# VectorE order in FF1: weight sums of a pair nearer to the pair, second-weight sums tied to the pairs' positions

## The chip, the cores and the metric

One Trainium2 chip, one of its cores. The metric is the device time of one execution in microseconds (us), lower is better. The kernel before took 1879.66 us (median of 3 runs, 1875.06 to 1884.38).

## The reference

One decoder layer on a sequence of 1024 tokens and a width of 1024. The first sublayer mixes tokens (sliding-window attention and a gated delta rule, side by side), the second is an MLP with 4096 hidden features. The change lies in the MLP's first product; everything ahead of it and the second product behind it are only neighbours.

```python
x = layer_norm(ALPHA * x + (1.0 + gt1) * mixed, ln1_g, ln1_b)     # end of the first sublayer
u2 = x * (1.0 + sc2) + sh2
h = jnp.square(jax.nn.relu(u2 @ w_ff1 + b_ff1))                    # FF1: (1024 x 1024) @ (1024 x 4096)
x = layer_norm(ALPHA * x + (1.0 + gt2) * (h @ w_ff2 + b_ff2), ln2_g, ln2_b)   # FF2
```

All of it is float32 from inputs to output.

## The kernel before, in words

**Number format.** Each float32 operand is split into a high part (ScalarE copies it to the matmul's type, line 215) and a low part (VectorE subtracts the high part from the source, line 216). A product is the sum of three matmuls: high by high, high by low, low by high.

**FF1 by seven products.** FF1 works on 16 pairs. Pair `i` is the two blocks of 128 hidden features `i` and `i + 16`. The product of 2 x 2 blocks (two halves of the 1024 inputs, two blocks of features, two halves of the tokens) is made from seven block products instead of eight, in the manner of Strassen and Winograd. That needs sums and differences of the weight blocks ahead of the products, and of the results behind them. Each product is 12 matmuls (4 slices of 128 by 3 split parts), so FF1 has 16 x 7 x 12 = 1344 matmuls of 128x512 on line 1869. From pair 5 on the products of a pair run in the order 1, 2, 6, 5, 7, 3, 4, and a pair takes 84 matmuls. Pairs 0 to 4 (`EARLY = 5`) are interleaved: products 1 and 2 of all five run first, then five products for each.

**Accumulators.** Products 1, 6, 7 and 4 of a pair add up in one PSUM bank (`mm`), 5 and 3 in another (`b`), product 2 has a third (`a`); in the first five pairs other banks take these parts. Because intermediate sums of a bank are results of their own, a bank is read in the middle: after product 5 ScalarE reads `b` (`part`, line 1587) before product 3 may go on in it, and after product 7 VectorE reads `mm` (`full`, line 1545) before product 4 may go on in it. TensorE waits at exactly these places when the reader is late.

**Results.** `part` copies a bank with the bias into a tile `t` (six of them rotate); `full` adds a bank to such a tile; `square` (lines 1595 and 1596) applies relu and square and stores the tile to `hf_d` in HBM through ScalarE's DMA queue; `last_block` (1606, 1607) does the same for product 4. `h_sums` and `h_sums2` (rows `sa`, `t`, `sb` on VectorE) make the sums of results that FF2 needs.

**First weights.** For each pair `f_load` (line 1541, SyncE's queue) brings two blocks of 512 KB (`fraw`). `f_alpha` splits the first as it is. Then `f_sums` makes `x` and an in-place sum (2 VectorE rows of 128x512), `f_sums2` makes two more in place (2 rows), and `f_gamma`, `f_beta`, `f_delta` split the changed blocks and `x`. Alpha serves products 1 and 2, gamma 6 and 3, beta 5 and 4, delta 7.

**Second weights.** FF2 uses seven products too. The sums of its weights are made during FF1: `t_load(n)` (lines 1691 to 1693, GpSimd's queue) loads 1 MB into `wx` (two tiles) and half of `sb`, `t_make(n)` makes four differences on VectorE (rows `wx<-wx` x3 and `sb<-sb,wx`, 128x512 each) and stores 4 x 256 KB to `wt_d` (line 1703, GpSimd's queue). There is one set of these buffers, so `t_load(n + 1)` writes where `t_make(n)` stored from.

**What sets the order.** The kernel writes every engine's queue itself. `at(p, f, ...)` puts an action at position `p`, and all actions up to `p` are written into the queues just ahead of the matmul with that number. `F0` is the number of FF1's first matmul, `pos[i, m]` that of product `m` of pair `i`. A position sets only the order of rows on an engine, not a time: each engine takes its rows strictly in that order, and waits for whatever a row depends on. Below, `b` is the position at which a pair begins, `pos[i, 1]`.

Of the kernel before, what the change touches and what calls it, by code (L numbers as in the profile page):

```python
# [34 lines left out]
def hybrid_layer_kernel(ctx: ExitStack, tc: tile.TileContext,  # L35
# [11 lines left out]
    V, A, G, T = nc.vector, nc.scalar, nc.gpsimd, nc.tensor  # L47
# [94 lines left out]
    NPAIR, EARLY = NF // 2, 5  # L142
# [54 lines left out]
    def at(p, f, *args):  # L197
        order[0] += 1
        heapq.heappush(events, (p, order[0], f, args))
# [325 lines left out]
    with tc.tile_pool(name="pa", bufs=2, side="right") as pa:  # L525
        if True:
            ba = pv.tile([P, NT, 16], F32, name="ba")
            for t in range(NT):
# [14 lines left out]
                if t:  # L543
                    vd = pa.tile([P, 4, 64], F32, tag="vd", name="vd", bufs=1)
                    a, b = (vraw, pv4) if t % 2 == 0 else (pv4, vraw)
# [106 lines left out]
        for h in range(8):  # L652
# [7 lines left out]
            for half in range(2):  # L660
                tp = psum("c", 1) if half else psum("b", 2)
                for j in range(4):
                    n = 4 * half + j
                    T.transpose(tp[:, j * P:(j + 1) * P], kT[:, n * P:(n + 1) * P], ident)
                for j in range(4):
                    n = 4 * half + j
# [16 lines left out]
            for half in range(2):  # L683
                kk = psum("a", 2)
                for j in range(4):
                    n = 4 * half + j
                    kc = kT[:, n * P:(n + 1) * P]
                    T.matmul(kk[:, j * P:(j + 1) * P], lhsT=kc, rhs=kc, start=True, stop=True)
                for j in range(4):
                    n = 4 * half + j  # L690
# [545 lines left out]
    for h in range(8):  # L1236
        b = Q0 + 144 * h
# [108 lines left out]
    F0 = E0 + 4 * SEG  # L1346
# [298 lines left out]
    pos = {im: F0 + 12 * n for n, im in enumerate(seq)}  # L1645
# [13 lines left out]
    for i in range(1, NPAIR):  # L1659
        if i < EARLY:  # L1660
            b = pos[i, 5]
            at(b - 70, f_load, i)
            at(b - (26 if i == 1 else 40), f_sums, i, V)
            at(b - (25 if i == 1 else 36), f_sums2, i, V)
            at(b - 17, f_beta, i)
            at(b - 3, f_gamma, i)
            at(b + 10, f_delta, i)
        else:
            b = pos[i, 1]
            at(b - 104, f_load, i)  # L1670
            at(b - (34 if i == EARLY else 76), f_alpha, i)
            at(b - (28 if i == EARLY else 66), f_sums, i, V)
            at(b - (27 if i == EARLY else 60), f_sums2, i, V)
            at(b + (8 if i == EARLY else -34), f_gamma, i)
            at(b + (26 if i == EARLY else -9), f_beta, i)
            at(max(b - (0 if i == EARLY else 22), pos[i - 1, 7] + 13), f_delta, i)
    for i in range(NPAIR):
# [25 lines left out]
            nc.gpsimd.dma_start(out=wt_d[j, n], in_=t)  # L1703

    for n in range(NPAIR):
        at(F0 + 110 + 76 * n, t_load, n)
        at(F0 + 146 + 76 * n, t_make, n)

# [117 lines left out]
    for s in range(7 * NS):  # L1828
        p = G0 + 24 * s
# [25 lines left out]
    for i, m in seq:  # L1855
# [8 lines left out]
        for k in range(4):  # L1864
            for x_ in range(3):
                run_events(count[0])
                (wh, wl), (uh_, ul_) = WF[i, w], U[mv]
                a, b = ((wh, uh_), (wh, ul_), (wl, uh_))[x_]
# [139 lines left out]
```

## Time and profile before

| | |
|---|---|
| time, median of 3 runs | 1879.66 us (1875.06 to 1884.38) |
| the profiled execution | 1881.81 us, of which the span from first to last instruction is 1880.1 us |
| TensorE clock granted, mean over the span | 0.990 |
| FF1's 1344 matmuls | from 1240.9 to 1561.0 us of the span |
| VectorE busy in the span | 1306.0 us (69%) |
| ScalarE busy in the span | 977.6 us (52%) |

All further times are microseconds from the start of the span. In rows of the timeline the first number is the start, the second the duration, then engine, line, operation, written tile `<-` read tiles, sizes and count; in square brackets stands how long the engine sat idle ahead of the row and what released it. A matmul of 128x512 is listed with 0.39 us, but they overlap: their starts are 0.227 us apart when nothing is in the way, so twelve of them, one product, take 2.72 us and a pair of 84 takes 19.04 us. `PE` is TensorE, `DVE` VectorE, `ACT` ScalarE, `POOL` GpSimd.

### The profile page before, as it was taken

The numbers are of one execution on the slowest core, as the hardware profiler recorded it, in microseconds if no ns is written. First come the engines' busy times: TensorE is split into PE (matmuls) and PEld (weight loads), VectorE is DVE, ScalarE is ACT, GpSimd is POOL, SyncE is SP. The second block draws the span as 40 slices with busy tenths as digits, with TensorE's granted clock in tenths as the row PEclk, the third lists the DMA queues.
The fourth block names the chain that finished last, engine by engine and source line by source line (L and its number), as shares of the span: only waits on it lengthen the run. The fifth ranks groups of instructions, "written<-read, shape, count | busy, mean of one in ns | idle before, by whom it ended". The sixth has DMA issues, their size and how long they took to land.

```text
span 1880.1 us, 26086 instructions
## 1 busy us (share of the span) xinstructions
PE 1826.4 (97%) x9161; PEld 1507.9 (80%) x9161; DVE 1306.0 (69%) x2473; ACT 977.6 (52%) x2105; POOL 339.2 (18%) x493
## 2 busy tenths in 40 slices
PE   7999999999999999999999999999999999999997
PEld 5877878878787878888878888877878787888886
DVE  7777588898875566666553445787867776576697
ACT  3689656666664454454553332465545555334441
POOL 7323323443331000000001110001221220000000
PEclk8999999999999999999999999999999999999999
DMA  9655642232248444544345644358978779755571
GB/s 260 171 183 199 214 100 77 84 98 70 68 170 227 127 139 134 159 149 144 118 157 187 205 141 151 123 168 279 311 240 282 261 244 396 281 196 170 198 259 45
DMA packets 262414, 337.74 MB, mean 180 GB/s; under 512 B 26005, under 2 KB 171110, under 8 KB 262026
## 3 DMA queue, kind: packets, MB, share of 16 engines
q1 hardware_dynamic: 222954, 212.94, 36.1%
q0 software_dynamic: 31328, 108.44, 17.1%
q10 hardware_dynamic: 8000, 14.68, 2.1%
q8 instruction: 72, 1.18, 0.3%
q14 instruction: 60, 0.49, 0.1%
HBM read 231.40 MB, written 102.51 MB: 178 GB/s over the span
## 4 chain that ended last, share of the span: by engine, by line
PE 77%; DVE 10%; DMA 5%; ACT 4%; issue 3%; SPq 1%; POOL 0%; ACTq 0%; DVEq 0%; POOLq 0%
PE mm L248 31%; PE mm L1929 6%; PE mm L1869 5%; PE b L1929 4%; PE a L1929 4%; PE b L1869 3%; PE c L1929 2%; PE a L1869 2%; PE mm L1499 2%; PE c L909 1%; DMA sraw<-in_w_ff_dram 1%; DVE wl L216 1%; PE mm L188 1%; PE mm L187 1%; PE mm L186 1%
## 5 line engine op out<-in xcount | busy, mean ns | idle before, releaser
L248 PE MATMUL mm<-uh,wl 128*128 128x512 f32 x800 | 332.3, 415 | 0.0
L248 PE MATMUL mm<-ul,wh 128*128 128x512 f32 x800 | 321.9, 402 | 0.0
L248 PE MATMUL mm<-uh,wh 128*128 128x512 f32 x800 | 318.4, 398 | 0.0
L216 DVE TENSOR_TENSOR sp<-sraw,sp 128x1024 fp32r<-128x1024 f32 x112 | 132.7, 1220 | 78.6 <-ACT sp L215 78.6
L215 ACT ACTIVATE sp<-sraw 128x1024 fp32r<-128x1024 f32 x112 | 112.8, 1054 | 124.0 <-PE b L1929 75.4
L248 PEld LDWEIGHTS mm<-ul,wh 128*128 128x128 f32 x800 | 151.4, 189 | 26.8 <-issue 0.2
L248 PEld LDWEIGHTS mm<-uh,wl 128*128 128x128 f32 x800 | 152.0, 190 | 23.1 <-issue 3.9
L248 PEld LDWEIGHTS mm<-uh,wh 128*128 128x128 f32 x800 | 151.7, 190 | 21.5 <-issue 0.2
L1929 PE MATMUL mm<-sp 128*128 128x512 f32 x528 | 137.3, 390 | 1.7 <-DVE sp L216 1.0
L1929 PEld LDWEIGHTS mm<-sp 128*128 128x128 f32 x528 | 98.4, 188 | 23.3 <-DVE sp L216 2.2
L216 DVE TENSOR_TENSOR wl<-wr,wh 128x1024 fp32r<-128x1024 f32 x81 | 98.6, 1218 | 7.5 <-ACT wh L215 7.5
L215 ACT ACTIVATE wh<-wr 128x1024 fp32r<-128x1024 f32 x81 | 85.1, 1050 | 22.0 <-PE c L1499 13.9
L1929 PE MATMUL a<-sp 128*128 128x512 f32 x336 | 92.6, 389 | 0.0
L1929 PE MATMUL b<-sp 128*128 128x512 f32 (+1 forms) x336 | 80.0, 374 | 0.0
L1169 ACT ACTIVATE vn<-a,brk 128x128 f32<-128x128 f32 x64 | 23.6, 368 | 108.1 <-PE a L1167 107.1
L842 DVE CUSTOM_DVE_ANT_0 nscore<-a,amask,nsink 128x256 f32<-128x256 f32 (+1 forms) x128 | 54.6, 464 | 34.6 <-PE a L835 33.8
L216 DVE TENSOR_TENSOR wl<-fraw,wh 128x1024 fp32r<-128x1024 f32 x43 | 52.5, 1222 | 35.5 <-ACT wh L215 35.2
L1929 PEld LDWEIGHTS a<-sp 128*128 128x128 f32 x336 | 63.1, 188 | 13.2
L853 POOL TENSOR_TENSOR sm<-sm 128x256 f32<-128x256 f32 x56 | 55.7, 994 | 99.0 <-ACT sm L849 66.2
L1929 PEld LDWEIGHTS b<-sp 128*128 128x128 f32 x336 | 60.5, 188 | 11.2
L849 ACT ACTIVATE sm<-nscore,stat 128x257 f32<-128x257 f32 (+1 forms) x128 | 62.1, 488 | 4.2 <-DVE stat L842 3.7
L894 POOL TENSOR_SCALAR_AFFINE_SELECT pl<-ph 128x512 fp32r<-128x512 f32 x56 | 44.0, 785 | 90.4 <-DVE ph L887 71.6
(524 smaller groups left out, 4678.0 us busy)
## 6 DMA issues: line engine op xcount, KB each, us to landing
wr<-in_w_in_dram SPq DMA_DIRECT2D x60, 512.0 KB, 3.6
sraw<-hf_d SPq DMA_DIRECT2D x54, 512.0 KB, 4.0
fraw<-in_w_ff_dram SPq DMA_DIRECT2D x32, 512.0 KB, 4.9
sraw<-wt_d SPq DMA_DIRECT2D x32, 512.0 KB, 4.4
hf_d<-t ACTq DMA_DIRECT2D x48, 256.0 KB, 4.2
wt_d<-wx POOLq DMA_DIRECT2D x48, 256.0 KB, 3.8
sraw<-in_w_ff_dram SPq DMA_DIRECT2D x22, 512.0 KB, 5.3
adaw<-in_w_ada_dram SPq DMA_DIRECT2D x41, 256.0 KB, 2.8
```

The costliest lines, as they stand in the source:

```text
L186: T.matmul(t, lhsT=wh[:, k, :], rhs=xh[k][:, sl], start=k == 0, stop=False)
L215: A.activation(out=hi, in_=src, func=AF.Copy)
L216: after(lag, lambda: V.tensor_tensor(out=lo, in0=src, in1=hi.bitcast(F32), op=ALU.subtract))
L248: T.matmul(ts[half], lhsT=w[:, k, :], rhs=xx[k][:, sl], start=k == 0 and m == 0, stop=k == KT - 1 and m == 2)
L842: V.tensor_tensor_reduce(out=ns[:, i, 1:1 + W], in0=sc[:, i * 2 * P:i * 2 * P + W], in1=amask[:, mo:mo + W], scale=-1.0, scalar=nsink[:, 2 ...
L849: A.activation(out=sm[:, i, 0:1 + W], in_=ns[:, i, 0:1 + W], func=AF.Exp, scale=-1.0, bias=st[:, i:i + 1], accum_out=st[:, 2 + i:3 + i])
L853: G.tensor_tensor(out=sm[:, :, 1 + P:1 + 2 * P], in0=sm[:, :, 1:1 + P], in1=sm[:, :, 1 + P:1 + 2 * P], op=ALU.add)
L894: G.affine_select(out=flat4(part), in_=flat4(full), pattern=[[0, 4], [1 if odd else -1, P]], compare_op=ALU.is_ge if odd else ALU.is_gt, f ...
L1169: after(1, lambda: A.activation(out=vn, in_=Wp[:, 0:P], func=AF.Copy, scale=brk[:, n, h:h + 1]))
L1499: T.matmul(pt, lhsT=m[k][:, tok], rhs=w[:, k % 2, :], start=k == 0 and w is wh and m is mh, stop=k == KT - 1 and m is ml)
L1869: T.matmul(pt, lhsT=a[:, k0 + k, :], rhs=b[k], start=begin and k == 0 and x_ == 0, stop=k == 3 and x_ == 2, skip_group_check=True)
L1929: T.matmul(to, lhsT=a[:, f, t * P:(t + 1) * P], rhs=b[:, f, lo:up], start=(begin or own) and s % NS == 0 and f == 0 and x_ == 0, stop=s % ...
```

## The change

Five numbers that set positions, and the rule for `t_load` and `t_make`:

```diff
             b = pos[i, 1]
             at(b - 104, f_load, i)
             at(b - (34 if i == EARLY else 76), f_alpha, i)
-            at(b - (28 if i == EARLY else 66), f_sums, i, V)
-            at(b - (27 if i == EARLY else 60), f_sums2, i, V)
-            at(b + (8 if i == EARLY else -34), f_gamma, i)
+            at(b - (28 if i == EARLY else 44), f_sums, i, V)
+            at(b - (27 if i == EARLY else 38), f_sums2, i, V)
+            at(b + (8 if i == EARLY else -30), f_gamma, i)
             at(b + (26 if i == EARLY else -9), f_beta, i)
             at(max(b - (0 if i == EARLY else 22), pos[i - 1, 7] + 13), f_delta, i)
...
     for n in range(NPAIR):
-        at(F0 + 110 + 76 * n, t_load, n)
-        at(F0 + 146 + 76 * n, t_make, n)
+        p = pos[n, 1] - 8 if n > EARLY else F0 + 100 + 68 * n
+        at(p, t_load, n)
+        at(p + 36, t_make, n)
```

From pair 6 on, `f_sums` and `f_sums2` are written 22 positions later and `f_gamma` 4 later. The second weights were done in a period of 76 positions, against 84 of a pair, so their place within a pair drifted. Now `t_make(n)` stands 28 positions behind the start of pair `n` for `n` of 6 and more; for `n` up to 5 the period is 68 and each comes 10 to 50 positions earlier than it did. What is computed stays the same, and so do all instructions, sizes and buffers. On TensorE, ScalarE, GpSimd and SyncE the rows keep their order; only VectorE's rows change places.

The first place is VectorE during pair 6 (`wl<-fraw,wh`: low part of alpha for pair 7; `x`, `fraw`: sums for pair 7; `t<-t,a`: `full` of product 2; `sb<-t,sa`: `h_sums2`; the second `wl`: low part of gamma for pair 7; `t<-t,mm`: `full` of product 7). Before:

```order
L216 TENSOR_TENSOR wl<-fraw,wh 128x1024
L1436 TENSOR_TENSOR x<-fraw 128x512
L1545 TENSOR_TENSOR fraw<-fraw 128x512
L1436 TENSOR_TENSOR sb<-t,sa 128x512
L1436 TENSOR_TENSOR wx<-wx 128x512 x3
L1436 TENSOR_TENSOR sb<-sb,wx 128x512
L1436 TENSOR_TENSOR fraw<-fraw 128x512 x2
L1545 TENSOR_TENSOR t<-t,a 128x512
L216 TENSOR_TENSOR wl<-fraw,wh 128x1024
L1545 TENSOR_TENSOR t<-t,mm 128x512
```

The same place now, and word for word the same in every pair from 6 to 14:

```order
L216 TENSOR_TENSOR wl<-fraw,wh 128x1024
L1436 TENSOR_TENSOR sb<-t,sa 128x512
L1545 TENSOR_TENSOR t<-t,a 128x512
L1436 TENSOR_TENSOR wx<-wx 128x512 x3
L1436 TENSOR_TENSOR sb<-sb,wx 128x512
L1436 TENSOR_TENSOR x<-fraw 128x512
L1545 TENSOR_TENSOR fraw<-fraw 128x512
L1436 TENSOR_TENSOR fraw<-fraw 128x512 x2
L216 TENSOR_TENSOR wl<-fraw,wh 128x1024
L1545 TENSOR_TENSOR t<-t,mm 128x512
```

`full` of product 2 has moved ahead of all eight sums; they stand between it and the low part of gamma.

The second place is VectorE later in pair 11, from `full` of product 2 to `full` of product 7. Before:

```order
L1545 TENSOR_TENSOR t<-t,a 128x512
L216 TENSOR_TENSOR wl<-fraw,wh 128x1024
L1436 TENSOR_TENSOR wx<-wx 128x512 x3
L1436 TENSOR_TENSOR sb<-sb,wx 128x512
L1545 TENSOR_TENSOR t<-t,mm 128x512
```

The last rows of the same stretch now:

```order
L1436 TENSOR_TENSOR x<-fraw 128x512
L1545 TENSOR_TENSOR fraw<-fraw 128x512
L1436 TENSOR_TENSOR fraw<-fraw 128x512 x2
L216 TENSOR_TENSOR wl<-fraw,wh 128x1024
L1545 TENSOR_TENSOR t<-t,mm 128x512
```

The second-weight sums no longer stand directly ahead of `full` of product 7; the low part of gamma does.

The third place is VectorE at the end of pair 4 of the first five, whose bank for products 1, 6, 7 and 4 is `b` (`t<-t,a`: `full` of product 3, `t<-t,b`: `full` of product 7, `wd`: low part of delta, `wl`: low part of gamma for pair 5). Before:

```order
L1436 TENSOR_TENSOR sb<-t,sa 128x512
L1545 TENSOR_TENSOR t<-t,a 128x512
L1545 TENSOR_TENSOR t<-t,b 128x512
L216 TENSOR_TENSOR wd<-x,wd 128x512
L216 TENSOR_TENSOR wl<-fraw,wh 128x1024
```

Now:

```order
L1436 TENSOR_TENSOR sb<-t,sa 128x512
L1545 TENSOR_TENSOR t<-t,a 128x512
L1436 TENSOR_TENSOR wx<-wx 128x512 x3
L1436 TENSOR_TENSOR sb<-sb,wx 128x512
L1545 TENSOR_TENSOR t<-t,b 128x512
L216 TENSOR_TENSOR wd<-x,wd 128x512
L216 TENSOR_TENSOR wl<-fraw,wh 128x1024
```

Here the four differences of `t_make(4)` have come to stand ahead of `full` of product 7.

## Prediction

> **What bounds the kernel now.** I read the page first, then who TensorE waits for in FF1, then windows of one pair each, then the rows around each wait.
>
> ```profile
> PE 1826.4 (97%) x9161; PEld 1507.9 (80%) x9161; DVE 1306.0 (69%) x2473; ACT 977.6 (52%) x2105; POOL 339.2 (18%) x493
> ...
> PE b L1869 <- ACT t L1587: 3.7, 2, 1.8
> PE mm L1869 <- DVE t L1545: 2.3, 2, 2.0
> PE mm L1869 <- ACT t L1587: 2.0, 2, 1.5
> ```
>
> TensorE is busy 97% of the span, and the change touches none of its rows. All it can win is TensorE's waiting. The other three lines list that for FF1: line 1869 waited six times for a reader of its own bank, 8.0 us in all (us in total, times, longest).
>
> ```profile
> 1362.55:1385.38 22.83, 20.98 (x86) 16.82 (x84) 13.93 (x19) 10.43 (x15) 3.78 (x7) 0.93 0.71 247
> 1385.38:1406.65 21.27, 19.43 (x85) 15.62 (x84) 14.33 (x20) 10.43 (x15) 3.78 (x7) 1.00 0.70 235
> 1406.65:1425.69 19.04, 19.04 (x85) 15.77 (x84) 13.83 (x20) 10.43 (x15) 3.77 (x7) 1.00 0.81 263
> ...
> 1463.77:1485.10 21.33, 19.34 (x86) 15.69 (x84) 15.40 (x21) 10.55 (x15) 4.48 (x9) 1.00 0.80 276
> ...
> 1378.15:1382.65 4.50, 4.49 (x13) 3.52 (x14) 2.42 (x3) 1.57 (x3) 0.00 (x0) 0.62 0.75 229
> ```
>
> Each row is a stretch: its length, busy time of PE, PEld, DVE, ACT and POOL, granted clock, share of the DMA engines, GB/s. The first four are pairs 6, 7, 8 and 11. Pair 8 takes 19.04 us with TensorE busy throughout, and so do pairs 9, 10 and 12 to 14. Pairs 6, 7 and 11 take 3.79, 2.23 and 2.29 us more, **8.31 us** together.
>
> **Why pairs 6 and 7 wait.**
>
> ```profile
> 1370.96 2.01 DVE L1436 TENSOR_TENSOR wx<-wx 128x512 f32<-128x512 f32 x3
> ...
> 1373.62 1.41 DVE L1436 TENSOR_TENSOR fraw<-fraw 128x512 f32<-128x512 f32 x2
> 1374.95 0.68 DVE L1545 TENSOR_TENSOR t<-t,a 128x512 f32<-128x512 f32 x1
> ...
> 1375.67 0.63 ACT L1595 ACTIVATE t<-t 128x512 f32<-128x512 f32 x1 [4.06 <-DVE t L1545]
> ...
> 1377.42 0.69 ACT L1587 ACTIVATE t<-b,cols 128x512 f32<-128x512 f32 x1 [0.46 <-ACT t L1596]
> ...
> 1375.92 0.39 PE L1869 MATMUL mm<-mh,wd 128*128 128x512 f32 x1
> 1378.16 0.50 PE L1869 MATMUL b<-u22h,wh 128*128 128x512 f32 x1 [1.84 <-ACT t L1587]
> ...
> 1379.70 0.63 PE L1869 MATMUL b<-u22h,wl 128*128 128x512 f32 x1
> ```
>
> In pair 6 the four `wx`/`sb` differences and the sums for pair 7 stand ahead of `full` of product 2 on VectorE. So it starts at 1374.95, though product 2 ended some 7 us before (24 of its matmuls behind 1362.55, at 0.227 us). ScalarE sits 4.06 us for it in `square`, and behind `square` in its queue stands the `part` that empties bank `b`. Product 3 could have started 0.23 us behind 1375.92; it starts at 1378.16, **2.01 us** late. Pair 7 repeats it: the two waits of `b` in the list, 3.7 us, are these two.
>
> **Why pair 11 waits.**
>
> ```profile
> 1478.86 2.01 DVE L1436 TENSOR_TENSOR wx<-wx 128x512 f32<-128x512 f32 x3
> ...
> 1481.51 0.68 DVE L1545 TENSOR_TENSOR t<-t,mm 128x512 f32<-128x512 f32 x1
> ...
> 1482.25 0.50 PE L1869 MATMUL mm<-mh,wh 128*128 128x512 f32 x1 [1.99 <-DVE t L1545]
> ```
>
> Here `t_make` has drifted to just ahead of `full` of product 7, which product 4 waits for; without it `full` could have taken the place of 1478.86. All three waits come from order on one engine, not from load: VectorE is busy 14 to 15 of 19 us.
>
> **The clock behind the wait.** Of pair 6's 3.79 us, 2.23 are the wait with its restart, as much as pair 7 lost in all. The other 1.56 us are slow matmuls: from 1379 to 1382.3 their starts are 0.43 instead of 0.227 us apart, and the granted clock over 4.5 us is 0.62. It follows one of three waits of 2 us, and no other stretch of FF1 that I read in pairs 5 to 15 has it, so I let it go with its wait. The Trainium skill (TensorE: Matmul & The Clock Gate, "HAM oscillation — how this bites in real kernels") warns only of idle gaps over about 3.4 us. A gap of 2.0 us would then have cost no clock, the 1.56 us would be chance, and my sum below would be smaller by them.
>
> **The change in a steady pair.** Pair 14 of before has the whole order in one undisturbed stretch, and gives every step.
>
> ```profile
> 1528.52 1.22 DVE L216 TENSOR_TENSOR wl<-fraw,wh 128x1024 fp32r<-128x1024 f32 x1
> 1529.66 0.69 DVE L1436 TENSOR_TENSOR x<-fraw 128x512 f32<-128x512 f32 x1
> 1530.38 0.69 DVE L1545 TENSOR_TENSOR fraw<-fraw 128x512 f32<-128x512 f32 x1
> ...
> 1531.59 1.41 DVE L1436 TENSOR_TENSOR fraw<-fraw 128x512 f32<-128x512 f32 x2
> 1532.92 0.68 DVE L1545 TENSOR_TENSOR t<-t,a 128x512 f32<-128x512 f32 x1
> 1533.51 2.01 DVE L1436 TENSOR_TENSOR wx<-wx 128x512 f32<-128x512 f32 x3
> 1535.56 0.69 DVE L1436 TENSOR_TENSOR sb<-sb,wx 128x512 f32<-128x512 f32 x1
> ...
> 1535.97 1.05 ACT L215 ACTIVATE wh<-fraw 128x1024 fp32r<-128x1024 f32 x1
> ...
> 1537.05 1.23 DVE L216 TENSOR_TENSOR wl<-fraw,wh 128x1024 fp32r<-128x1024 f32 x1 [0.80 <-ACT wh L215]
> ...
> 1539.50 0.39 PE L1869 MATMUL mm<-mh,wh 128*128 128x512 f32 x1
> ```
>
> I count from the pair's start, 1523.18. The low part of alpha starts at 5.34, and the next row 1.14 later. In the new order that is `sb` (6.48), then, 0.61 on, `full` of product 2 at 7.09. ScalarE gets it at 7.8, not at 10.4, and `part` of product 5 waits for nothing but product 5 (48 matmuls, 10.9), so the wait of pairs 6 and 7 cannot recur. The four `t_make` rows take 7.69 to 10.35 (1533.51 to 1535.56, and 0.61). The sums follow: `x` at 10.35, `fraw` at 11.07, the last two from 11.79 to 13.20. Gamma's high part on ScalarE needs them: 13.24 to 14.29. Its low part starts at 14.32, `full` of product 7 at 15.46 and ends at 16.14; 0.06 more for the hand-over (pair 11: ends 1482.19, matmul 1482.25) gives 16.20. Product 4 starts at 16.32 by the last row. So pair 11's wait goes as well, in every pair, but **only 0.12 us** of slack stay, where `full` ended at about 15.7 before. I charge 0.5 us for jitter on nine pairs; the bounds are 0 and, with 0.2 us each, 2.
>
> **Loads.** GpSimd's queue keeps its order, and a load of second weights goes out when its buffer's store has landed:
>
> ```profile
> 1376.46 0.54 POOL L1692 DMA_DIRECT2D wx<-in_w_ff_dram  x1 [1.39 <-DMA wt_d<-wx]
> ```
>
> So the new position of `t_load` does nothing by itself; loads come earlier only because `t_make` does. The row stands 5.5 us behind its `t_make` (1370.96). The last of such loads goes out a little later and takes this long (KB each, median us to landing, pairs 6 to 14):
>
> ```profile
> sb<-in_w_ff_dram POOLq DMA_DIRECT2D x9, 256.0 KB, 6.4
> ```
>
> So some 12 to 13 us pass, against 19.04 between two `t_make`: hidden. The `fraw` buffer is freed 0.4 us later than before, while the sums that need its next load moved back 4 us.
>
> **The first five pairs.**
>
> ```profile
> 1271.10:1340.79 69.69, 66.79 (x288) 53.77 (x289) 57.18 (x79) 37.52 (x55) 14.02 (x26) 1.00 0.88 299
> ...
> 1310.00:1340.00 30.00, 29.47 (x129) 24.17 (x130) 25.00 (x35) 17.15 (x25) 6.02 (x12) 1.00 0.97 339
> ...
> 1300.52 0.50 PE L1869 MATMUL mm<-mh,wh 128*128 128x512 f32 x1 [0.33 <-DVE t L1545]
> ...
> 1302.13 7.56 DMA hf_d<-t
> ...
> 1334.59 1.06 ACT L215 ACTIVATE wh<-fraw 128x1024 fp32r<-128x1024 f32 x1 [0.40 <-ACT t L1607]
> ...
> 1336.01 1.22 DVE L216 TENSOR_TENSOR wl<-fraw,wh 128x1024 fp32r<-128x1024 f32 x1
> ...
> 1340.53 0.68 DVE L1545 TENSOR_TENSOR t<-t,a 128x512 f32<-128x512 f32 x1
> ...
> 1343.51 0.39 PE L1869 MATMUL b<-mh,wh 128*128 128x512 f32 x1
> ```
>
> TensorE idles 2.9 us in the 69.7 us of the first row. One wait (0.6 us with its restart, at 1300.52) is for `full` behind `t_make(1)`; that `t_make` now stands 18 positions, 4 us, earlier and ahead of rows that wait for others: **-0.6**. The 2.0 us of `mm` behind line 1587 in the first list, 2.4 with restarts, are waits for `part`, whose tile is still being stored; the store of 1302.13 takes 7.56 us. These depend on how full the DMA engines are (0.97 in the second row), and the change packs 68 positions of second weights where 76 were. I leave that at 0; the bounds are -2.4 and, if each of pairs 1 to 4 waits as long as the longest did (1.5, with restart 1.7), 4 x 1.7 - 2.4 = +4.4.
>
> One wait is **new**. At the end of pair 4, `t_make(4)` now stands ahead of `full` of product 7. The row at 1336.01 can start at 1335.69 (end of the high part, plus 0.04), so `full` of product 3 at 1340.21, `t_make(4)` at 0.60 later until 1343.46, and `full` of product 7 ends at 1344.14. Product 4, due at 1343.51, starts at 1344.20: 0.7, with restart **+0.8**. Its bounds are 0 and 2, if the load of `t_make(4)` lands 1.2 us late.
>
> **Sum.** -8.3 (pairs 6, 7, 11) -0.6 +0.8 +0.5 = -7.6. Against the profiled execution, 1881.81, that is 1874.2. The median of the runs is 2.15 lower, and the runs spread over 9.3, so I carry the difference over: 1879.66 - 7.6 = **1872.0**. What FF2 starts with is unmoved: the last `t_make` stands 28 positions behind its pair's start, where it stood 26.
>
> **Rivals.**
> - *Crowded DMA in the first pairs* gives back +4.4 and another +1.2 at pair 4: 1872.0 + 5.6 = 1877.6. For it speaks the 0.97; against it that `t_make(1)` and `t_make(2)` leave the time of the slow stores. The rule that speaks against this change is in the Trainium skill (DMA: Bandwidth & Descriptors, "Issuing engines are not separate DMA queues"): DMAs of all issuing engines run interleaved on the same 16 engines, so a separate queue for second weights protects no store.
> - *The opposite:* the early stores shorten as well, -2.4, and the jitter costs nothing: 1872.0 - 2.9 = 1869.1.
> - *Slower:* the chain sums, gamma high, gamma low, `full` runs over its 0.12 us. Place: product 4 of the nine pairs 6 to 14. If every one waits as long as pair 11 did, 9 x 2.29 = 20.6 stand in place of the 0.5: 1892.1. It decides from 0.9 us a pair (8.1 over 9); for that, something in the chain must be a microsecond longer than in pair 14. Nothing in the rows is.
> - *The order is not the cause:* the waits stay, moved to a late store. Then 1879.7. The 4.06 us released by VectorE speak against it.
>
> **How the numbers follow.** Forecast 0.50, crowded 0.20, opposite 0.19, slower 0.04, not the cause 0.07. The range from 1866.5 to 1878.5 takes in the opposite case and most of the crowded one, with some 2 us for the median of a few runs. A measurement of this kernel can tell about 0.5% from no change, that is 9.4 us: faster than that needs below 1870.3, which is the opposite case (0.17) and the forecast's lower part (0.15): 0.32. Slower by as much: 0.05. The rest, 0.63, is a gain too small to tell.
>
> **What would show it.** Pairs 6 to 14 at 19.04 us each, with `full` of product 2 at 7.1 and `full` of product 7 at about 15.5 behind the pair's start; clock 1.00 throughout; a wait of about 0.7 us for `t` line 1545 at pair 4. Wrong would be: waits on line 1545 before product 4 in pair after pair (slower), or longer waits on line 1587 before 1340 (crowded).

## The result, and the profile after

The changed kernel took **1865.03 us** (median of 4 runs, 1863.83 to 1868.29), beside 1881.5 us for the kernel before on the same chip: ratio **0.9917** (its time over that of the kernel before; **95% interval 0.9896 to 0.9938**). Measured twice more beside the kernel before it gave 0.9941 (0.9920 to 0.9962; 1869.18 us) and 0.9941 (0.9928 to 0.9955; 1870.50 us). It is faster by 0.6 to 0.8%: 11 us by the two repeats, 16 by the first measurement. The forecast was 1872.0, a gain of 7.6, with a range down to 1866.5. The first measurement lies 1.5 us below that range, the repeats lie in its lower half.

The page of the changed kernel gives busy time, share of the span and instructions of each engine:

```profile
PE 1820.0 (98%) x9161; PEld 1503.1 (81%) x9161; DVE 1306.0 (70%) x2473; ACT 976.9 (52%) x2105; POOL 338.5 (18%) x493
```

VectorE is busy as long as before, 1306.0 us. Nothing became shorter; what went is waiting. The list of who TensorE waits for (us in total, times, longest) has three lines left in which FF1's matmuls wait for the reader of their bank:

```profile
PE b L1870 <- DVE t L1545: 0.8, 2, 0.5
PE mm L1870 <- ACT t L1587: 0.7, 1, 0.7
...
PE b L1870 <- ACT t L1587: 0.6, 1, 0.6
```

That is 2.1 us in four waits, all of them in matmuls of the first five pairs, where it was 8.0 us in six. The windows of pairs 6, 7, 8 and 11, with the columns of the prediction:

```profile
1355.45:1374.53 19.08, 19.08 (x85) 15.71 (x84) 13.92 (x19) 10.44 (x15) 4.10 (x8) 1.00 0.95 318
1374.53:1393.60 19.07, 19.07 (x85) 15.71 (x84) 13.92 (x19) 10.44 (x15) 3.78 (x7) 1.00 0.78 257
1393.60:1412.66 19.06, 19.06 (x85) 15.71 (x84) 13.92 (x19) 10.44 (x15) 3.79 (x7) 1.00 0.73 249
...
1450.83:1469.89 19.06, 19.06 (x86) 15.70 (x84) 13.93 (x19) 10.44 (x15) 3.78 (x7) 1.00 0.79 259
```

The three long pairs (22.83, 21.27 and 21.33 us) are as short as the others, and the clock stays at 1.00. VectorE's rows in pair 6, which begins at 1355.45, show why:

```profile
1361.94 0.68 DVE L1436 TENSOR_TENSOR sb<-t,sa 128x512 f32<-128x512 f32 x1
1362.54 0.68 DVE L1545 TENSOR_TENSOR t<-t,a 128x512 f32<-128x512 f32 x1
1363.14 2.01 DVE L1436 TENSOR_TENSOR wx<-wx 128x512 f32<-128x512 f32 x3
1365.18 0.69 DVE L1436 TENSOR_TENSOR sb<-sb,wx 128x512 f32<-128x512 f32 x1
1365.79 0.68 DVE L1436 TENSOR_TENSOR x<-fraw 128x512 f32<-128x512 f32 x1
...
1367.24 1.42 DVE L1436 TENSOR_TENSOR fraw<-fraw 128x512 f32<-128x512 f32 x2
1369.78 1.22 DVE L216 TENSOR_TENSOR wl<-fraw,wh 128x1024 fp32r<-128x1024 f32 x1 [1.13 <-ACT wh L215]
1370.92 0.68 DVE L1545 TENSOR_TENSOR t<-t,mm 128x512 f32<-128x512 f32 x1
```

`full` of product 2 starts 7.09 us behind the pair's start (forecast 7.09), the differences at 7.69 (7.69), `x` at 10.34 (10.35), `full` of product 7 at 15.47 (15.46). No row between them waits, but for the 1.13 us in which VectorE waits for gamma's high part, which TensorE does not feel.

**Where the time went, by parts.** One profile of each kernel would mislead here, so this table has three of each; every figure is a difference between the starts of two matmuls of one profile, or between a matmul's start and an end of the span. The difference is the mean of after less the mean of before.

| part | before, three profiles | after, three profiles | difference | forecast |
|---|---|---|---|---|
| FF1's first matmul starts at | 1240.93, 1233.18, 1241.01 | 1233.62, 1233.29, 1239.70 | -2.8 | 0 |
| first five pairs | 99.86, 100.34, 101.28 | 99.24, 100.07, 99.75 | -0.8 | -0.6 |
| pair 5 (with product 4 of pair 4) | 21.76, 21.76, 21.76 | 22.59, 22.58, 22.60 | +0.8 | +0.8 |
| pairs 6 to 14 | 179.67, 178.16, 182.84 | 171.64, 171.60, 171.89 | -8.5 | -8.3 + 0.5 |
| pair 15 to the end of the span | 337.88, 340.16, 338.61 | 336.21, 336.16, 336.46 | -2.6 | 0 |

FF1 up to pair 15 gained 8.5 us where 7.6 was forecast. Two rows are forecast as nothing and are not nothing: the part ahead of FF1, whose instructions are the same in the same order, and the part from pair 15 on.

### The profile page after: what moved, and what is told of

The parts are those of the page before. It is cut to its first block, busy times and chain, and to the rows that moved or that the text cites. A ratio compares the mean times of both kernels' runs of the same rounds, so it can differ in the third digit from the quotient of the medians.

```text
span 1863.3 us, 26105 instructions
## 1 busy us (share of the span) xinstructions
PE 1820.0 (98%) x9161; PEld 1503.1 (81%) x9161; DVE 1306.0 (70%) x2473; ACT 976.9 (52%) x2105; POOL 338.5 (18%) x493
## 4 chain that ended last, share of the span: by engine, by line
PE 77%; DVE 9%; ACT 4%; DMA 3%; issue 2%; POOL 0%; ACTq 0%; SPq 0%; POOLq 0%; DVEq 0%
PE mm L248 32%; PE mm L1870 7%; PE mm L1930 6%; PE b L1930 4%; PE a L1930 4%; PE b L1870 3%; PE a L1870 2%; PE mm L1499 2%; PE c L1930 2%; PE c L909 2%; PE a L1499 1%; DVE wl L216 1%; PE mm L188 1%; PE mm L187 1%; PE mm L186 1%
## 5 line engine op out<-in xcount | busy, mean ns | idle before, releaser
L248 PEld LDWEIGHTS mm<-uh,wh 128*128 128x128 f32 x800 | 151.2, 189 | 21.3 <-issue 0.2
L215 ACT ACTIVATE wh<-fraw 128x1024 fp32r<-128x1024 f32 x43 | 45.0, 1055 | 33.2 <-PE b L1870 16.3
```

The lines of the kernel that those rows point to most:

```text
L215: A.activation(out=hi, in_=src, func=AF.Copy)
L248: T.matmul(ts[half], lhsT=w[:, k, :], rhs=xx[k][:, sl], start=k == 0 and m == 0, stop=k == KT - 1 and m == 2)
```

## The experiments

### Both kernels again

No edit. The first comparison of profiles had 7.3 of its 16.8 us ahead of FF1, where nothing was changed. Is that the program or the execution?

> The kernel before, unchanged, profiled once more. The profiled execution of after gained 16.8 us of span: 7.31 ahead of the first matmul of the first product (1240.93 against 1233.62), 7.82 between there and the second product, 1.67 behind it. Theory A (the part ahead is not the change's: it differs between executions of one and the same program, by when DMAs land): the ratio is 1.00, and the first matmul of the first product comes at a time that lies some microseconds away from 1240.9, anywhere from 1233 to 1245, while the pairs again take 21.8, 22.8, 21.3, 19.04 x3, 21.3, 19.04 x3. Rival B (the part ahead belongs to the changed program, for instance by where its instructions lie): the first product begins within 1 us of 1240.9 again. Both: the first product takes 320 us, within 1.

> The changed kernel, unchanged, profiled once more. Theory A: the ratio is again 0.992 within 0.003, the first product begins anywhere from 1230 to 1242 us. Rival B: it begins within 1 us of 1233.6. Both: the first product takes 312.5 us within 1, pairs 6 to 14 19.05 to 19.1 us each.

> The kernel before a third time, for the parts whose size differs between executions. Theory (which waits there are is fixed by the order, but how DMAs land and whether the clock falls is chance): the first product begins between 1233 and 1241 us (1240.9 and 1233.2 so far), three waits of 2.0 to 2.2 us in pairs 6, 7 and 11, each followed by 1.5 us of slow matmuls or by none (8 of 18 such waits so far), and 337.5 to 340.5 us from pair 15's start to the end. Rival (the first profile is typical and the second was not): it begins at 1240 to 1242. Ratio 0.998 to 1.002.

> The changed kernel a third time. Theory: the first product begins between 1233 and 1241 us, so that the 1233.6 and 1233.3 so far are chance; FF1 312.5 to 313.5; 336.0 to 336.5 from pair 15's start to the end. Rival (something of the change moves the begin): 1233.5 again, within 0.5. Ratio 0.991 to 0.995.

The kernel before against itself gave ratios of 1.0003 (0.9991 to 1.0015) and 1.0000 (0.9986 to 1.0014). FF1 began at 1233.18, then at 1241.01; with the changed kernel at 1233.29, which by itself would have fitted rival B, then at 1239.70, which does not. The view of one line's instructions gives the matmuls just ahead of FF1 (fastest, median and slowest duration in ns, then first and last start). In the first profile of before:

```profile
L1499 PE MATMUL mm<-wh,mh x64: 388/389/477, 1145.7 to 1231.2; 128*128 128x512 f32 x64
```

In the second profile of the same kernel:

```profile
L1499 PE MATMUL mm<-wh,mh x64: 388/389/477, 1138.1 to 1223.4; 128*128 128x512 f32 x64
```

The same program reaches the same matmul 7.6 us earlier in one execution than in the other, while the time from the first to the last start differs by 0.2 us (85.5 and 85.3). So the begin of FF1 varies by up to 7.8 us between executions of one program, and theory A holds: the 7.3 us were no effect of the change. That the kernel before takes 320 us for FF1 and 22.8 us for pair 6 each time was a miss: FF1 took 320.3, 321.0 and 324.9 us. In the third profile pairs 6, 7 and 11 took 22.81, 22.85 and 22.93 us, where the second had 21.27, 21.29 and 21.37; the run with both jobs ahead shows what that is.

Half of the 7.6 us comes from one place long before FF1. In the first profile TensorE waited there, and the granted clock behind the wait was 0.50 for 3.4 us (the third number from the right is the clock):

```profile
596.86 0.41 PE L1145 MATMUL b<-ident,vT 128*128 128x128 f32 x2 [2.03 <-DVE E L1131]
...
597.45:600.87 3.42, 3.42 (x10) 2.64 (x9) 1.46 (x3) 1.78 (x6) 0.56 (x1) 0.50 1.08 225
```

In the second profile the same matmuls did not wait, and behind them the first profile was 3.7 us further back. About 3 us of the rest arose in the first 590 us and 1.0 at 959 us, where one wait for ScalarE was 1.28 us long in the first profile and 0.26 in the second. Why VectorE was late for line 1145 in one execution stays open.

### One half of the change alone

The first with only the positions of `f_sums`, `f_sums2` and `f_gamma`, the second with only those of `t_load` and `t_make`:

```diff
-            at(b - (28 if i == EARLY else 66), f_sums, i, V)
-            at(b - (27 if i == EARLY else 60), f_sums2, i, V)
-            at(b + (8 if i == EARLY else -34), f_gamma, i)
+            at(b - (28 if i == EARLY else 44), f_sums, i, V)
+            at(b - (27 if i == EARLY else 38), f_sums2, i, V)
+            at(b + (8 if i == EARLY else -30), f_gamma, i)
```

> Only the pair sums of the first weights (and gamma) move; the loads and sums of the second weights stay at their fixed spacing of 76. Theory (two jobs together ahead of product 2's quantisation are what makes pairs 6, 7 and 11 late, either one alone fits): pairs 6 to 14 take 19.05 to 19.1 each, pair 5 about 23.0 (22.6 in after), the first five as in before; first product about 313 us, 7 less than before, ratio about 0.993 to 0.996. Rival (only both moves together remove the waits): one or two of pairs 6, 7, 11 still take 21 or more; first product 315 to 318. Of the part ahead of the first product theory A says that it varies by itself, rival B that this program has a begin of its own.

```diff
-        at(F0 + 110 + 76 * n, t_load, n)
-        at(F0 + 146 + 76 * n, t_make, n)
+        p = pos[n, 1] - 8 if n > EARLY else F0 + 100 + 68 * n
+        at(p, t_load, n)
+        at(p + 36, t_make, n)
```

> Only the loads and sums of the second weights move, tied to the pairs; the pair sums of the first weights stay 66 ahead. Theory (either half alone is enough): pairs 6 to 14 take 19.05 to 19.1 each, pair 5 about 23.7, the first five as in after; first product 313 to 314 us, ratio 0.993 to 0.997. Rival (the sums of the first weights are what is late, whatever the second weights do): pairs 6, 7 and 11 or all of 6 to 14 take 20 to 22.8; first product 318 us or more, ratio 0.998 to 1.005.

What the first expectation calls product 2's quantisation is its `full`. With the sums only, the ratio was 0.9945 (0.9932 to 0.9959), pairs 6 to 14 took 19.04 to 19.09 us, pair 5 22.76 and FF1 314.1. With the second weights only, it was 0.9954 (0.9941 to 0.9967), pairs 6 to 14 took 19.04, pair 5 23.69 and FF1 314.4. **Either half alone removes all three waits.** In pairs 6 and 7 neither the sums nor `t_make` is too much for its place; both together are. In pair 11 either half brings the differences ahead of the low part of gamma: they start 15.1 us behind the pair's start in before, and 10.5 and 10.3 us with one half moved. Each half alone has a wait in pair 5 for `full` (0.7 and 0.8 us) which neither the kernel before nor the changed one has. FF1 came out 1.1 and 0.4 us longer than expected. Unexpected was the end: from pair 15's start it took 336.5 us with the sums moved, as in after, but 339.6 with only the second weights moved, as in before.

### The sums of the last pair

One pair's sums moved in the kernel before, and the same pair's sums put back in the changed one:

```diff
-            at(b - (28 if i == EARLY else 66), f_sums, i, V)
+            at(b - (28 if i == EARLY else 44 if last else 66), f_sums, i, V)
...
-            at(b - (28 if i == EARLY else 44), f_sums, i, V)
+            at(b - (28 if i == EARLY else 66 if last else 44), f_sums, i, V)
```

(`last` is `i == NPAIR - 1`; `f_sums2` and `f_gamma` alike.)

> The kernel before with the sums of one pair alone moved, those for pair 15 (the last), so that in pair 14 the differences of the second weights come 2.7 us earlier and stand ahead of those sums. From the first matmul of pair 15 to the end of the span it took 337.9 and 340.2 us in two profiles of before, 339.6 with only the second weights moved, but 336.2, 336.2 and 336.5 in the three with the sums moved. Theory (this one place does it: the four stores of those differences and the last loads of second weights leave the queues before the first loads of the second product go out, which then land earlier): 336.0 to 336.8 here, no wait of the first split on its load longer than in after, first load of the second product landed by 11.7 us behind pair 15's start; pairs 6, 7 and 11 still 21.3 or more. Rival (the whole new order of FF1, or chance): 337.5 to 340.5. Ratio 0.997 to 1.000.

> The changed kernel with the sums for pair 15 alone put back where they were. Theory: pairs 6 to 14 stay at 19.05 to 19.1 us, and from pair 15's start to the end it takes 338 to 340.5 again instead of 336.2. Rival: 336.2 stays. Ratio 0.993 to 0.997, against 0.9917 and 0.9941 of the changed kernel.

The first kernel, last early, took 336.53 us from pair 15's start (ratio 0.9985, 0.9971 to 0.9998), with pairs 6, 7 and 11 late as before. The second, last late, took 339.12 us (0.9954, 0.9939 to 0.9970), with pairs 6 to 14 short. So **this one place makes the 2.6 us** behind pair 15. GpSimd's queue shows the path. Before (pair 15 begins at 1542.22):

```profile
1534.49 1.15 POOL L1703 DMA_DIRECT2D wt_d<-wx  x2 [12.21 <-DVE wx L1436]
...
1541.31 0.54 POOL L1692 DMA_DIRECT2D wx<-in_w_ff_dram  x1 [3.70 <-DMA wt_d<-wx]
1542.32 0.54 POOL L1693 DMA_DIRECT2D sb<-in_w_ff_dram  x1 [0.46 <-PE mm L1869]
```

With the last pair's sums moved (pair 15 begins at 1539.97):

```profile
1529.56 1.15 POOL L1703 DMA_DIRECT2D wt_d<-wx  x2 [9.51 <-DVE wx L1436]
...
1534.44 0.54 POOL L1692 DMA_DIRECT2D wx<-in_w_ff_dram  x1 [1.76 <-DMA wt_d<-wx]
1535.68 0.54 POOL L1693 DMA_DIRECT2D sb<-in_w_ff_dram  x1 [0.70 <-DMA wt_d<-sb]
```

The stores of `t_make(14)` start 7.7 us ahead of pair 15 in the first, 10.4 ahead in the second, and the last load goes out 0.1 us behind its start against 4.3 ahead of it. FF2's first loads (`sraw`) go out 2.9 us behind it in both. By then the last load of second weights has landed in the second (1.8 us behind pair 15's start), but not in the first (5.5). The first `sraw` takes 9.4 us to landing in the first and 7.5 in the second. ScalarE's first split of what they bring, before:

```profile
1554.52 1.06 ACT L215 ACTIVATE sp<-sraw 128x1024 fp32r<-128x1024 f32 x1 [0.54 <-DMA sraw<-hf_d]
```

And with the last pair's sums moved:

```profile
1551.63 1.05 ACT L215 ACTIVATE sp<-sraw 128x1024 fp32r<-128x1024 f32 x1
```

It starts 12.30 us behind pair 15's start and is released by a DMA in the one, and 11.66 us behind it, waiting for nothing, in the other; in last late it is 13.6 us. The run of the next section has these stores earlier still, 13.4 us ahead of pair 15, with the sums where before has them, and takes 335.9 us. So what counts is when the differences are stored, not where the sums stand. Over all profiles, the five with the stores 7.7 us ahead take 337.9 to 340.2 us from pair 15's start, the nine with earlier stores 334.9 to 337.1.

### Both jobs ahead of `full`, in every pair

The run with only the second weights moved, with one number changed:

```diff
-        p = pos[n, 1] - 8 if n > EARLY else F0 + 100 + 68 * n
+        p = pos[n, 1] - 14 if n > EARLY else F0 + 100 + 68 * n
```

> The run with only the second weights moved, and their differences 6 positions earlier still: in every pair from 6 to 14 the four differences and the sums stand ahead of product 2's full, as in pair 6 of before. Theory (8 differences and sums ahead of full, 5.3 us, make product 3 wait 2.0 us and restart in 0.23): nine pairs of 21.2 to 21.4 us, FF1 about 334 us against 314.4, ratio 1.005 to 1.009. Whether waits of 2.0 us pull the granted clock down: by the one case in four so far (1.56 us of slow matmuls) two or three of the nine pairs take 22.8; if it was chance without a link to the wait, none. Rival (load, not order): the pairs stay at 19.05 or wait under 1 us.

The ratio was 1.0077 (1.0053 to 1.0100). Pairs 6 to 14 took 199.05 us against 171.36, with nine waits. The list of who TensorE waits for has them, with one more of the first five pairs:

```profile
PE b L1870 <- ACT t L1587: 17.3, 10, 1.8
```

Six positions on one engine's list cost 27.7 us (`t_load` moves with them).

The granted clock does not fall behind every wait. Read in steps of 3.413 us that begin where the clock changes, it is 1.00 or 0.50 in a whole step. Here are the steps with the first and the fourth wait, each with the next one (the first number behind the comma is TensorE's busy time, the third from the right the clock):

```profile
1371.37:1374.79 3.41, 1.57 (x7) 1.03 (x6) 0.61 (x2) 2.28 (x4) 1.13 (x3) 1.00 0.89 275
1374.79:1378.20 3.41, 3.41 (x9) 2.65 (x9) 2.42 (x3) 1.13 (x2) 0.00 (x0) 0.50 0.73 238
...
1439.64:1443.05 3.41, 1.71 (x7) 1.42 (x8) 0.78 (x1) 2.66 (x4) 1.08 (x2) 1.00 0.90 254
1443.05:1446.46 3.41, 3.41 (x16) 2.68 (x15) 3.41 (x5) 2.22 (x3) 0.00 (x0) 1.00 0.79 250
```

All nine gaps between matmuls are 1.99 to 2.01 us, yet five pairs take 22.8 us and four 21.3. The first wait lies whole in one step and leaves TensorE 1.57 us of work in it; the clock of the next step is 0.50. The fourth begins 0.30 us ahead of a step and leaves 1.71 us in it; the clock stays. 9 x 2.23 + 5 x 1.53 = 27.7 us, which is the whole loss. I had expected two or three falls in nine, by one case in four; with pair 11's waits it was one in six by then.

### The differences of pairs 3 and 4

What is left in FF1 of the changed kernel, in TensorE's rows of the first profile:

```profile
1315.79 0.50 PE L1870 MATMUL b<-mh,wd 128*128 128x512 f32 x1 [0.62 <-ACT t L1587]
1321.84 0.50 PE L1870 MATMUL b<-mh,wh 128*128 128x512 f32 x1 [0.31 <-DVE t L1545]
1336.27 0.50 PE L1870 MATMUL b<-mh,wh 128*128 128x512 f32 x1 [0.52 <-DVE t L1545]
```

The third is the new wait that the prediction put at +0.8. The second and third should go if `t_make(3)` and `t_make(4)` stand behind `full`. Three kernels: both, pair 4 alone, pair 3 alone.

```diff
-        at(p + 36, t_make, n)
+        at(p + {3: 46, 4: 40}.get(n, 36), t_make, n)     # both
+        at(p + {4: 40}.get(n, 36), t_make, n)            # pair 4
+        at(p + {3: 46}.get(n, 36), t_make, n)            # pair 3
```

> The changed kernel with the differences of the second weights of pairs 3 and 4 put behind product 7's full (10 and 4 positions later). Theory (the waits of 0.57 and 0.79 us before the products that reuse that bank come from the four differences ahead of full): both waits go, pair 5 takes 21.8 instead of 22.6, FF1 311.2 to 312.0 instead of 312.5 and 313.3, and nothing else moves by over 0.1 us. Rival (full would be late anyway, for its bank or for ScalarE): at least one of the two waits stays with over 0.3 us. A gain of 1.4 us is below what the times can tell; ratio 0.990 to 0.995.

> The changed kernel with only the differences of pair 4 put 4 positions later, behind product 7's full; SyncE's order is that of the changed kernel. In the run with pairs 3 and 4 the two waits went, but the first five pairs took 102.1 us instead of 99.2 and 100.1, since the wait of a part for its store grew (2.0 us before pair 4's product 6, none before). Theory (that came from pair 3's half, which pulled a load of 256 KB ahead of two stores in SyncE's queue): first five 99.2 to 100.4, pair 5 21.76, so FF1 311.7 to 312.6, best of all. Rival (it came from pair 4's half or is chance): first five over 101.

> The changed kernel with only the differences of pair 3 put 10 positions later; SyncE issues the load of t ahead of two stores, as in the run with both. Theory: the wait of 0.57 us goes, but part of product 6 in pair 4 waits for its store by 1.5 to 2.5 us on TensorE; first five 101 to 102.5, pair 5 22.6. Rival (the longer wait was chance or pair 4's): first five 98.7 to 100.

With both, the ratio was 0.9932 (0.9912 to 0.9952). The two waits went and pair 5 took 21.76, but the first five pairs took 102.14 us and FF1 314.6, which was a miss. ScalarE's row for `part` of pair 4's product 6 shows what came instead:

```profile
1331.60 0.69 ACT L1587 ACTIVATE t<-b,cols 128x512 f32<-128x512 f32 x1 [3.85 <-DMA hf_d<-t]
```

It waits for the store of the tile that it is to overwrite; in the second profile of the changed kernel it did not wait. SyncE's queue had changed with it, now:

```profile
1318.61 5.77 SPq L1541 DMA_DIRECT2D fraw<-in_w_ff_dram  x2
1324.48 0.97 SPq L1612 DMA_DIRECT2D t<-hf_d  x1
1326.00 0.34 SPq L1583 DMA_DIRECT2D hf_d<-t  x1
1326.72 0.57 SPq L1622 DMA_DIRECT2D hf_d<-sa  x1
```

In the changed kernel's second profile:

```profile
1318.45 5.37 SPq L1541 DMA_DIRECT2D fraw<-in_w_ff_dram  x2
1325.43 0.34 SPq L1583 DMA_DIRECT2D hf_d<-t  x1
1326.16 0.37 SPq L1622 DMA_DIRECT2D hf_d<-sa  x1
1326.64 0.68 SPq L1612 DMA_DIRECT2D t<-hf_d  x1
```

A load of 256 KB had come to stand ahead of two stores. Pair 3 alone repeats it, with 0.9942 (0.9921 to 0.9963), a wait of 2.09 us at the same place and 101.17 us for the first five (pair 5 took 21.76, not 22.6; that TensorE, held up there, gave VectorE its time is argued, not shown). Pair 4 alone gave 0.9931 (0.9914 to 0.9947; 1868.69 us), first five 98.43, pair 5 21.76, and **FF1 310.9 us, the shortest of all** and shorter than expected, against 313.3 of the changed kernel in the same set of runs. Of that, 0.84 us is the wait taken away; 1.3 us are shorter waits of `part` for stores (0.32 and 0.48 us in place of 0.91 and 1.20), which differ between executions. In time the two cannot be told apart (0.9931 and 0.9941). That the load ahead of the stores is what delays them fits all three kernels, but `t_make(3)`'s own stores moved with it, and no run moved the load alone.

## Why the prediction was wrong, step by step

- **Pairs 6, 7 and 11 (-8.3): right.** Order on VectorE, not load, made them late: both halves of the change remove the waits, one by one (19.04 us), and the order of pair 6 put into nine pairs makes nine waits of 2.0 us.
- **The clock behind the wait (1.56 of the 8.3): right to count, wrong to call a single event.** "It follows one of three waits of 2 us": over the three profiles of before it followed one, none and three of three; with last early and both ahead, 11 of the 21 waits of 2.0 to 2.2 us in pairs 6 to 14. Three waits cost 3 x 11/21 x 1.53 = 2.4 us of it in a mean execution. That the one profile the forecast rests on had one fall, near this mean, was luck. The Trainium skill (TensorE: Matmul & The Clock Gate, "HAM oscillation — how this bites in real kernels") warns only of gaps over about 3.4 us; the nine equal gaps of 2.0 us, five of them with a step of 0.50 behind them, show that a gap well below that can cost clock too.
- **`t_make(1)` (-0.6) and the first five pairs: right.** The wait for `full` behind `t_make(1)` is gone. The means differ by -0.8 us, but waits for stores vary by more than that (0.7, 1.6 and 0.9 us for the first of them in three profiles of after). The crowded rival did not come.
- **The new wait of pair 4 (+0.8): right.** Pair 5 took 0.83 us more in all three profiles, the wait is for line 1545, and 4 positions take it away.
- **Jitter in nine pairs (+0.5): half as much.** Over three profiles 26 of 27 pairs took 19.06 to 19.09 us and one 19.37. The slack of 0.12 us was enough in 26 (product 4 started 16.32 us behind the pair's start, in the one at 16.51), and the slower rival did not come.
- **"What FF2 starts with is unmoved": wrong, and this step is why the gain is larger.** I looked at the last `t_make`, which moved by 2 positions. But the one ahead of it, `t_make(14)`, comes 2.7 us earlier in its pair, because the sums for pair 15 that stood ahead of it now stand behind it. The prediction worked this out for `full` and dropped it for the stores that hang on `t_make`, though it says that "loads come earlier only because `t_make` does". The last loads of second weights have then landed before FF2's first loads go out, and these land sooner. That is worth 2.6 us, which the sum put at nothing, shown from both sides by the two runs on the last pair. Without it 1865.03 would have been 1867.6, inside the forecast range.
- **The part ahead of FF1, forecast as 0: the size of the first measurement.** The forecast -7.6, with the 2.6 and the 0.9 that FF1 gained more, makes -11.1, which is what both repeats measured (0.9941 of 1881 is 11.1 less). The first measurement has by its ratio some 4.5 us more. Its profile has FF1 beginning at 1233.6; the executions of both kernels begin it anywhere from 1233 to 1241. That its runs fell to the early side would explain it. With the 630 us that the three profiles of after take from FF1's first matmul to the end, the spans of its four runs (1863.3, 1862.1, 1866.6, 1863.4) put the begin at about 1233, 1232, 1237 and 1233; this is an estimate, and only the first of the four was profiled. In one profile of before half of the spread is the wait at line 1145 with its slow clock; what makes the rest is open.

## What to carry to other kernels

Where engines take rows in a list's order, ask of each wait which two jobs stand ahead of the late row; moving either may do, and it is enough to move the one whose own result has slack. When a job moves past another, follow everything that hangs on the other as well, its stores and what they free, up to the next stage's first loads. And compare profiles stage by stage with a second profile of the unchanged kernel beside them: here the begin of FF1, behind identical instructions, differed by 7.8 us, as much as the effect sought.

## What was not expected of the hardware

Gaps of 2.0 us in TensorE's work pulled the granted clock down in 11 of 21 cases, and each time it cost about 1.5 us (pairs of 22.77 to 22.93 us, against 21.24 to 21.37 where it stayed up). The Trainium skill (TensorE: Matmul & The Clock Gate, "What's actually happening") describes a window of 3413 ns that runs freely, so that the point at which the clock changes depends on where in it the first matmul lands. The traces here agree. In the run with nine equal waits the steps of clock 0.50 begin at 1374.79, 1398.68, 1463.53, 1507.90 and 1552.28; they are 7, 19, 13 and 13 times 3.413 us apart.

So the place of a wait within such steps can be read from the profile. In FF1 of all 14 profiles, TensorE worked 1.41 to 1.57 us in the eleven steps that were followed by a clock of 0.50, and 1.71 us or more in every other (where FF1 has no such fall, the steps are laid out from the falls elsewhere in the profile). The eleven waits with a fall lie in one step, two of them but for 0.1 us. The ten without, and the waits of 2.01 and 2.09 us at `part` of pair 4's product 6 in the two runs that move `t_make(3)`, all lie across the border of two steps. A wait of 2.0 us that falls anywhere lies whole in a step of 3.413 us in (3.41 - 2.0)/3.41 = 41% of cases, and nearly whole in some more; this estimate fits 11 of 21. Whether the clock falls is thus chance for a kernel of this kind, while its odds hang on the length of the wait. No run moved a wait within a step on purpose. And ahead of FF1, where other matmuls run, the border is not the same: in the run with nine waits a step from 234.74 with 1.91 us of work was followed by a clock of 0.50.
